# Eighteen small unused GpSimd loads beside a softmax that keeps VectorE and the DMA engines full

## The chip, the cores and the metric

One core of a Trainium2 chip. The metric is device microseconds of one execution of the whole program. A span in the profile is the same execution by the profiler's clock, about 1.8 us shorter.

## The reference

Softmax over the last axis of a float32 array of 16 x 1024 x 512, with temperature 0.5:

```python
def reference(x):
    temp = 0.5
    x_scaled = x / temp
    x_max = np.max(x_scaled, axis=-1, keepdims=True)
    exp_x = np.exp(x_scaled - x_max)
    return (exp_x / np.sum(exp_x, axis=-1, keepdims=True)).astype(np.float32)
```

33.55 MB are read and 33.55 MB written; the arithmetic is small beside that.

## The kernel before

The 16,384 rows are cut into eight chunks of 128 partitions x 16 rows x 512 (4.19 MB each). Six buffers hold chunks; the loads of the last two chunks wait until the stores of the first two have left theirs. VectorE takes the maximum and makes the bias, ScalarE the exponentials with their sums, VectorE the reciprocal and the product (ScalarE takes an eighth of that), and a store in place follows. Loads go out on SyncE's queue, stores on ScalarE's.

```python
    def load(c):
        if c < BUFS:
            chunks[c] = data.tile([P, G, D], fp32, name="xt")
        else:
            chunks[c] = chunks[c - BUFS]
        xt = chunks[c]
        for lo, hi in LOADS[c]:
            nc.sync.dma_start(out=xt[:, lo:hi, :], in_=xr[c][:, lo:hi, :])
    # ... shift, exponentials, scale_vector, scale_scalar: the arithmetic of one block
    def store(i):
        c, _, end = blocks[i]
        for lo, hi in STORES[c]:
            if hi == end:
                nc.scalar.dma_start(
                    out=outr[c][:, lo:hi, :], in_=chunks[c][:, lo:hi, :]
                )
    # ... the pipeline over 11 blocks: shift two ahead, exponentials one ahead, store(i) last
```

## Time and profile before

| | before |
|---|---|
| time, median of 2 runs | 162.37 us (162.31 to 162.43) |
| span of the profiled run | 160.6 us |
| VectorE busy | 134.6 us (84%) |
| DMA engines, both big queues | 97.7% of the span |
| last store issued / its landing time | 147.55 us / 12.2 us |

One group more matters later, from the groups of instructions of the kernel before (busy us, mean ns, then idle time ahead of it): the bias, which is the one VectorE operation that could meet GpSimd.

```profile
L78 DVE TENSOR_SCALAR bias<-negmax 128x16 f32<-128x16 f32 (+2 forms) x11 | 1.9, 173 | 0.4
```

### The profile page before, as it was taken

The page shows a single profiled execution, that of the slowest core. Times are in us where ns is not written, and L with a number is a line of the kernel's source. Part 1 is how long each engine was busy: PE and PEld are TensorE (multiplying, and loading weights), DVE is VectorE, ACT ScalarE, POOL GpSimd, SP SyncE. Part 2 cuts the span into 40 slices and gives each one's busy share as a digit, 9 for nine tenths or more (in the row PEclk, how much of TensorE's full clock was granted, in tenths as well). Part 3 has the DMA queues.
Part 4 walks back from the last instruction along what each step waited for, and adds up shares of the span by engine and source line. Part 5 has one row for each costly group of instructions (what it writes and reads, how often), then busy time and mean ns, then how long its engine had stood idle before and what let it go on. Part 6 is the DMA issues. An engine that isn't in the chain of part 4 may idle for free.

```text
span 160.6 us, 402 instructions
## 1 busy us (share of the span) xinstructions
DVE 134.6 (84%) x45; ACT 102.1 (64%) x273; POOL 0.2 (0%) x4
## 2 busy tenths in 40 slices
DVE  0507999999999999999999999999999999957000
ACT  3071549069979963998199909991899891790000
POOL 0000000000000000000000000000000000000000
DMA  5999999999999999999999999999999999999993
GB/s 182 471 400 506 400 400 498 408 392 484 424 400 384 400 457 449 400 441 465 400 424 473 408 408 492 400 392 498 416 392 490 424 392 457 457 392 449 465 392 139
DMA packets 2450, 67.13 MB, mean 418 GB/s; under 512 B 272, under 2 KB 272, under 8 KB 272
## 3 DMA queue, kind: packets, MB, share of 16 engines
q1 hardware_dynamic: 1296, 33.56, 49.3%
q10 hardware_dynamic: 1152, 33.55, 48.4%
q14 instruction: 2, 0.02, 0.0%
HBM read 33.55 MB, written 33.55 MB: 418 GB/s over the span
## 4 chain that ended last, share of the span: by engine, by line
DVE 80%; DMA 7%; ACT 4%; issue 0%; SPq 0%
DVE negmax L74 42%; DVE xt L102 36%; DMA xt<-in_x_dram 7%; ACT xt L85 4%; DVE bias L78 1%; DVE recip L100 1%; SPq L66 0%
## 5 line engine op out<-in xcount | busy, mean ns | idle before, releaser
L85 ACT ACTIVATE xt<-xt,bias 128x512 f32<-128x512 f32 x128 | 90.4, 708 | 41.7 <-DVE bias L78 41.2
L74 DVE TENSOR_REDUCE negmax<-xt 128x16 f32<-128x8192 f32 (+2 forms) x11 | 69.9, 6352 | 9.5 <-DMA xt<-in_x_dram 9.5
L102 DVE TENSOR_TENSOR xt<-xt,recip 128x7168 f32<-128x7168 f32 (+2 forms) x11 | 62.0, 5637 | 0.4
L85 ACT ACTIVATION_READ_ACCUMULATOR xt<-xt,bias 128x1 f32 x128 | 23.9, 187 | 0.0
L111 ACT ACTIVATE xt<-xt,recip 128x512 f32<-128x512 f32 x15 | 9.9, 706 | 0.0
L100 DVE RECIPROCAL recip<-sums 128x16 f32<-128x16 f32 (+2 forms) x11 | 2.4, 218 | 1.8 <-ACT xt L85 1.8
L78 DVE TENSOR_SCALAR bias<-negmax 128x16 f32<-128x16 f32 (+2 forms) x11 | 1.9, 173 | 0.4
L52 ACT ACT_TABLE_LOAD x1 | 1.3, 1283 | 0.7 <-PEq L148 0.7
L51 DVE MEMSET warm<- 128x1 f32 x1 | 0.1, 59 | 0.8 <-PEq L148 0.8
L52 ACT ACTIVATE warm<-warm 128x1 f32<-128x1 f32 x1 | 0.2, 203 | 0.0
L148 POOL MEMSET const-bfloat16-1.0<- 128x1 bf16 x1 | 0.1, 103 | 0.0
L148 POOL MEMSET const-uint8-127<- 128x1 uint8 x1 | 0.1, 103 | 0.0
L148 POOL MEMSET const-float32-1.0<- 128x1 f32 x1 | 0.1, 100 | 0.0
L148 POOL MEMSET const-float32-0.0<- 128x1 f32 x1 | 0.1, 99 | 0.2 <-issue 0.2
## 6 DMA issues: line engine op xcount, KB each, us to landing
out_dram<-xt ACTq DMA_DIRECT2D x8, 4096.0 KB, 22.8
xt<-in_x_dram SPq DMA_DIRECT2D x7, 4096.0 KB, 30.2
xt<-in_x_dram SPq DMA_DIRECT2D x1, 3072.0 KB, 11.7
xt<-in_x_dram SPq DMA_DIRECT2D x1, 1024.0 KB, 4.9
```

Source lines behind the costliest of these rows:

```text
L51: nc.vector.memset(warm, 0.0)
L52: nc.scalar.activation(out=warm, in_=warm, func=EXP)
L74: nc.vector.tensor_reduce(negmax[:, 0:b], chunks[c][:, lo:hi, :], axis=AX, op=MAX, negate=True)
L78: nc.vector.tensor_scalar_mul(biases[i][:, 0:b], negmax[:, 0:b], 2.0)
L85: nc.scalar.activation(out=row, in_=row, func=EXP, bias=biases[i][:, g : g + 1], scale=2.0, accum_out=sums[i][:, g : g + 1],)
L100: nc.vector.reciprocal(recips[i][:, 0:b], sums[i][:, 0:b])
L102: nc.vector.tensor_mul(rows, rows, recips[i][:, 0:k].unsqueeze(2).broadcast_to((P, k, D)))
L111: nc.scalar.activation(out=row, in_=row, func=COPY, scale=recips[i][:, g : g + 1])
L148: nc = _bacc.Bacc("TRN2", target_bir_lowering=False, num_devices=1)
```

## The change

It adds loads that no one reads, each of the six in a round of a size of its own, so that they can be told apart in a record of DMA packets. They are called markers here. Each round has markers of 2, 4 and 8 partitions with one row each, and of 1, 1 and 14 partitions with two rows each. Nothing else is touched.

```diff
         xt = chunks[c]
+        if c in (1, 5, 6):
+            mark_pool()
         for lo, hi in LOADS[c]:
             nc.sync.dma_start(out=xt[:, lo:hi, :], in_=xr[c][:, lo:hi, :])
+
+    junk = stats.tile([16, 2, D // 2], fp32, name="junk", bufs=1)
+
+    def first(n, size):
+        nc.gpsimd.dma_start(out=junk[0:n, 0, 0:size], in_=xr[0][0:n, 0, 0:size])
+
+    def turn(n, size):
+        nc.gpsimd.dma_start(
+            out=junk[0:n, :, 0:size], in_=xr[0][0:n, 0:2, 0:size]
+        )
+
+    def mark_pool():
+        first(2, 250)
+        first(4, 240)
+        first(8, 230)
+        turn(1, 220)
+        turn(1, 210)
+        turn(14, 200)
```

## The prediction

> **What bounds the kernel now.** I read the page first (busy shares, the row of slices, DMA queues), then the chain that ended last, then the landing times of the DMA issues, and last the stretches of the tail. From the page:
>
> ```profile
> span 160.6 us, 402 instructions
> DVE 134.6 (84%) x45; ACT 102.1 (64%) x273; POOL 0.2 (0%) x4
> DVE  0507999999999999999999999999999999957000
> POOL 0000000000000000000000000000000000000000
> DMA  5999999999999999999999999999999999999993
> DMA packets 2450, 67.13 MB, mean 418 GB/s; under 512 B 272, under 2 KB 272, under 8 KB 272
> q1 hardware_dynamic: 1296, 33.56, 49.3%
> q10 hardware_dynamic: 1152, 33.55, 48.4%
> ```
>
> Two rows are full at once. VectorE is at 9 from the fifth slice to the 35th, and the DMA engines are at 9 from the second slice to the 39th. The two queues together take 49.3 + 48.4 = 97.7% of the engines' time. GpSimd does nothing after four constants. So there are two candidates for the bound, and the chain tells which one sets the end:
>
> ```profile
> DVE 80%; DMA 7%; ACT 4%; issue 0%; SPq 0%
> 1.15 11.71 DMA xt<-in_x_dram
> 12.88 2.30 DVE negmax L74
> 143.59 3.89 DVE xt L102
> ```
>
> VectorE starts in earnest at 12.88 us, when the second load of the first chunk lands, and goes on to 147.48 us (143.59 + 3.89) with one wait of 1.8 us for ScalarE. Then the last store goes out. What follows is pure DMA:
>
> ```profile
> 147.55 0.34 ACTq L119 DMA_DIRECT2D out_dram<-xt  x1
> DMA to landing us min/median/max: 12.2/22.8/32.4
> xt<-in_x_dram SPq DMA_DIRECT2D x1, 1024.0 KB, 4.9
> 144.00:146.00 2.00, 2.00 (x1) 0.54 (x1) 0.00 (x0) 1.00 0.76 328
> ```
>
> The second line is the least, middle and longest landing time of the eight stores, each 4.194 MB; 147.55 + 12.2 = 159.75, against a span of 160.6, so the shortest is that of the last store. Set beside the very first load, which found the engines empty (1.049 MB, 4.9 us), it gives a straight line: (12.2 - 4.9) / (4.194 - 1.049) = 2.32 us per MB, or 431 GB/s, and 4.9 - 1.049 x 2.32 = 2.5 us that do not depend on size. The last store therefore found no backlog that this line would show, and the DMA share of 0.76 just before it says the same. Conclusion: the end is the first load (12.88) + VectorE's chain (134.6) + one store alone (12.2) and about 1 us around them. The DMA engines are a near second: they finish what was queued just as the last store arrives, so a DMA loss over the whole run has hardly any slack to hide in.
>
> **What the Trainium skill says.** First, "DMA: Bandwidth & Descriptors", section "Why a DMA increments its semaphore by 16 and not by 1": a DMA issued by GpSimd has all 16 engines post the completion, whatever its shape, while its data go to k consecutive engines from a cursor that moves on. The trace agrees on the 16 as far as it goes: 17 DMAs x 16 = 272, just the count of packets under 512 B. The cursor, no line of the kernel before shows. Second, same page, "Queues, rings and completion order": each engine goes round its queues packet by packet. In the trace a data packet is a 32 KB row (33.55 MB over 1,024 rows in q10), which at 431 / 16 = 26.9 GB/s takes 1.22 us; that is my unit for one turn of another queue. Third, same page, "Anatomy of one DMA": a GpSimd DMA costs some 2.0 us fixed, mostly completion; my line has 2.5 us for the other queues. Fourth, "SBUF — State Buffer", section "Who interferes with whom": descriptor generation on GpSimd is kept out, or keeps VectorE out, only where VectorE is in a mode that uses both port pairs, which tensor_reduce and tensor_tensor are not said to have; a tensor_scalar can. Here that is the 11 small multiplications that make the bias, 0.17 us each. No run here shows such a conflict yet.
>
> **The change, part by part.** It removes nothing and moves nothing. VectorE, ScalarE and SyncE have the same instructions with the same waits in the built program; only GpSimd gets 18 DMAs. It looks as if the three rounds belonged to the loads of chunks 1, 5 and 6, but GpSimd has no wait on these loads. All 18 write the same scratch tile, so each but the first waits for the completion of the one before, and nothing else. The series starts right after the start barrier, near 0.8 us, and runs on by itself; no one waits for it except the end of the kernel.
>
> *Bytes.* One round: 2 x 1000 + 4 x 960 + 8 x 920 + 2 x 880 + 2 x 840 + 28 x 800 B = 39,040 B in 46 rows. Three rounds: 0.117 MB in 138 rows, 0.17% of 67.13 MB. At 431 GB/s that is 0.27 us if spread evenly. If the cursor works as the skill says, a round covers 2 + 4 + 8 + 2 + 2 + 14 = 32 shares, each engine twice, so evenly it is.
>
> *Packets.* 138 data and 18 x 16 = 288 completions = 426 on top of 2450, or 27 per engine beside 153. What does a small one cost? The only hint before: q1 has 144 packets more than q10 for 0.01 MB more, and 0.9% more of the engines' time, which is 0.009 x 160.6 x 16 / 144 = 0.16 us each. Most of these 144 are the first chunk's extra data rows, and one queue reads HBM while the other writes it, so this is a ceiling. With 0.02 us each (my choice, an estimate), 27 make 0.5 us per engine; the ceiling would make 4.3 us.
>
> *On the path.* About a tenth of the series runs before 12.88 us, so the first load loses some 0.05 us. VectorE's chain loses time only if a bias multiplication meets descriptor generation. Taking 1 us of GpSimd per DMA (estimate), 18 us in 160 is a chance of 0.11 each; 11 x 0.11 x about 0.5 us = 0.6 us if every overlap blocked, and I count a third, 0.2 us. The DMA loss of 0.27 + 0.5 us is hidden while VectorE sets the pace and reaches the end only as backlog in front of the last store; I count a third, 0.25 us. Sum: 0.05 + 0.2 + 0.25 = 0.5 us, so 162.37 + 0.5 = 162.9 us.
>
> **The rivals.**
> *The series outlasts the kernel.* A marker that lands slowly makes the 18 in series long. Its time is 2.5 us fixed, about 1 us to make descriptors, and turns behind 32 KB packets: until the first store at 45.6 us only loads are queued (1.22 us a turn), later both queues (up to 2.44 us). If a marker's rows and completion go as one packet, that is 4.7 to 5.9 us, and the series ends near 18 x 5.5 = 99 us, far from the end. If each row and the completion need a turn of their own, up to three turns, it is 7.2 us early and up to 10.8 us late: six markers by 45 us, twelve more at 8.5 us on average, end near 147 us. The edge is 160 / 18 = 8.9 us each. Above it, markers are left when the last store lands, each at about 3.5 us: at 10 us each two are left, +7 us, about 169 us (4% slower). For it: both queues are full nearly throughout. Against: waits for a whole turn on every descriptor are the worst case. I give it 0.13.
> *Small packets cost their ceiling.* 4.3 us per engine, not hidden because the engines are full: about 166 us, 2% slower. Against: 272 such packets are there already without denting the 0.98 to 1.03 shares of the middle stretches. Weight 0.04, half of it past 2%.
> *Wholly hidden.* The markers fill gaps, VectorE feels nothing, 162.4 us. The likeliest neighbour of my figure, 0.4.
> *Faster?* Nothing is removed, and no order changes; only chance in which queue goes first could gain, tenths of a us. 0.01.
>
> **Range and chances.** Same within 2% is 159.1 to 165.6 us. From the above: slower 0.13 x 0.7 + 0.04 x 0.5 = 0.11, rounded to 0.12 for an added fixed cost of a third queue at the end of the program, which I cannot size; faster 0.01; within 2% 0.87. The range that should hold it 8 times in 10 is lopsided for the same reason: 162.2 to 165.2 us, and the figure is 162.9 us.
>
> **What would show it.** In the profile after: 426 more packets (2876), all under 2 KB, in a third queue with well under 1% share; 288 of them under 512 B. VectorE's groups keep their times (tensor_reduce of 8192 elements 8.68 us, the multiplication of 7168 7.63 us), and bias near 0.17 us with at most one or two stretched. The last store is issued within 1 us of 147.55 and lands in 12.2 to 13 us. The markers land in 5 to 9 us each and the last before 150 us. I am wrong if the chain of work ends in a marker or in GpSimd; if VectorE shows new idle time before a group; if the last store lands in more than 14 us; or if the loads of the first chunk land over half a us later than 12.88.

## The result, and the profile after

163.62 us (163.56 to 163.68, 2 runs) against 162.37 us: ratio 1.0078, interval 1.0058 to 1.0098. A ratio is the mean time of one kernel's fast runs over that of the other's of the same rounds, so not quite the ratio of the medians quoted. The time is inside the range forecast, 0.7 us above the figure.

The page after, the lines that answer to those in the prediction:

```profile
span 161.9 us, 424 instructions
DVE 134.6 (83%) x45; ACT 102.1 (63%) x273; POOL 10.1 (6%) x22
DMA packets 3026, 67.25 MB, mean 415 GB/s; under 512 B 752, under 2 KB 848, under 8 KB 848
q1 hardware_dynamic: 1296, 33.56, 49.0%
q10 hardware_dynamic: 1152, 33.55, 48.0%
q0 software_dynamic: 576, 0.12, 0.4%
L100 DVE TENSOR_SCALAR bias<-negmax 128x16 f32<-128x16 f32 (+2 forms) x11 | 1.9, 173 | 0.4
```

VectorE's 134.6 us and the bias's 173 ns have not moved: GpSimd didn't hold VectorE up. The new queue q0 has 576 packets, not the 426 of the prediction, and 0.4% of the engines' time. 576 is 18 x 32. The packet records of the trace, which give sizes and times but don't name the engines, show where they come from: 96 packets carry rows, and 480 have 4 or 8 bytes. 18 x 16 = 288 of the small ones are the completions; that leaves 192, and 96 + 192 = 288 is again 16 per marker. So it looks as if each engine that got no row got a small filler packet instead.

The chain of waits after, the store's landing times (least, middle, longest) and the markers' landing times:

```profile
1.16 11.76 DMA xt<-in_x_dram
143.64 3.89 DVE xt L124
DMA to landing us min/median/max: 13.0/24.2/33.4
DMA to landing us min/median/max: 4.9/7.3/9.8
136.98 0.62 POOL L78 DMA_DIRECT2D junk<-in_x_dram  x1 [6.97 <-DMA junk<-in_x_dram]
```

The first chunk lands at 12.92 in place of 12.86 us, and VectorE ends at 147.53 in place of 147.48. The last store is the one with the least landing time, and that rose from 12.2 to 13.0. The 18 markers ran one behind the other and the last was issued at 137.0 us, so the series was over at 144.7 us, before the kernel's end.

That leaves a part which neither chain shows: after the last store had landed. This is SyncE in the trace records, start times in us, from the last landing to the end:

```
before  landed 159.71  waits 159.77 159.83                                            end barrier 159.89  span ends 160.57
after   landed 160.57  waits 160.58 160.65 160.71 160.77 160.83 160.89 160.95 161.01 161.08  end barrier 161.14  span ends 161.90
```

A completion semaphore is a counter that a DMA raises when its data have landed. The program ends with SyncE waiting for every one that was used, up to two of them in one instruction. The first start listed for the changed kernel is that of the wait which the last store ends; the same one of the kernel before is not in its line, because its record starts at 140.43 us. Behind that wait stand two more before and eight after. In the new kernel eight semaphores belong to GpSimd's markers; they had been full for about 16 us, yet six waits with one of them stand behind the last store's, and each takes 0.06 us although there is nothing to wait for. From the last landing to the end it is 0.85 us before and 1.33 us after: 0.39 us of the difference lies before the end barrier, in these waits, and 0.08 us in the barrier itself (0.67 us before, 0.76 after), where GpSimd's clearing of the semaphores takes 0.14 us in place of 0.09.

So the span's 1.33 us come apart like this, each from one profile:

| part | before | after | difference |
|---|---|---|---|
| last store issued | 147.55 | 147.61 | +0.06 |
| last store to its landing (records) | 12.16 | 12.96 | +0.80 |
| last landing to the end of the span | 0.85 | 1.33 | +0.47 |

The packet records also tell why the landing moved. In the kernel before, from 5 us to the issue of the last store, each engine was without a packet for only about 0.1 us in all, so there was no gap in which the markers could hide. In the changed kernel their packets took 0.60 us an engine, and the ends of the last 16 rows, averaged, moved from 158.35 to 159.07 us, by 0.72. The difference of 0.12 is within the scatter: in the run *one* below, with 0.02 us of marker packets, that average is 158.71 us.

### The profile page after: what moved, and what is told of

The parts are those of the page before. It is cut to its first block, busy times and chain, and to the rows that moved or that the text cites. A ratio compares the mean times of both kernels' runs of the same rounds, so it can differ in the third digit from the quotient of the medians.

```text
span 161.9 us, 424 instructions
## 1 busy us (share of the span) xinstructions
DVE 134.6 (83%) x45; ACT 102.1 (63%) x273; POOL 10.1 (6%) x22
## 4 chain that ended last, share of the span: by engine, by line
DVE 79%; DMA 7%; ACT 4%; issue 0%; SPq 0%
DVE negmax L96 41%; DVE xt L124 36%; DMA xt<-in_x_dram 7%; ACT xt L107 4%; DVE bias L100 1%; DVE recip L122 1%; SPq L68 0%
## 5 line engine op out<-in xcount | busy, mean ns | idle before, releaser
L78 POOL DMA_DIRECT2D junk<-in_x_dram x9 | 5.0, 553 | 66.8 <-DMA junk<-in_x_dram 66.8
L75 POOL DMA_DIRECT2D junk<-in_x_dram x9 | 4.9, 543 | 60.5 <-DMA junk<-in_x_dram 59.6
```

What stands on the lines that cost most here:

```text
L75: nc.gpsimd.dma_start(out=junk[0:n, 0, 0:size], in_=xr[0][0:n, 0, 0:size])
L78: nc.gpsimd.dma_start(out=junk[0:n, :, 0:size], in_=xr[0][0:n, 0:2, 0:size])
```

## The experiments

**Theories.** A: the DMA engines are a full second bound, so the markers' engine time comes back nearly whole at the last store, and the end waits come on top. B: the slow series, still running near the end, is what hurts; early losses would be made up. C: a third queue costs a flat sum as soon as it is used. Two more came up with the results, D (a burst among loads alone puts the engines out of step) and E (the uneven share of rows does). Runs of one call were taken on the same chip with 11 runs of the kernel before (medians 162.27, 162.33 and 162.33 us in the three calls).

| run | median us | ratio (interval) | VectorE ends | last store to landing | landing to end |
|---|---|---|---|---|---|
| before (first profile) | 162.37 | | 147.48 | 12.16 | 0.85 |
| changed (first profile) | 163.62 | 1.0078 (1.0058 to 1.0098) | 147.53 | 12.96 | 1.33 |
| again | 163.57 | 1.0084 (1.0070 to 1.0098) | 147.46 | 13.48 | 1.33 |
| one | 162.53 | 1.0018 (1.0002 to 1.0035) | 147.24 | 12.51 | 0.99 |
| same8 | 163.18 | 1.0057 (1.0041 to 1.0073) | 147.50 | 12.22 | 1.32 |
| burst18 | 164.14 | 1.0111 (1.0098 to 1.0124) | 147.66 | 13.38 | 1.33 |
| late18 | 163.68 | 1.0089 (1.0074 to 1.0103) | 147.35 | 13.06 | 1.33 |
| even18 | 163.59 | 1.0076 (1.0064 to 1.0088) | 148.06 | 12.36 | 1.32 |
| merged | 163.03 | 1.0044 (1.0031 to 1.0058) | 148.68 | 11.50 | 0.99 |
| short (wrong) | 161.21 | 0.9928 (0.9917 to 0.9940) | 147.28 | 11.10 | 0.85 |
| shortmarks (wrong) | 161.81 | 0.9969 (0.9957 to 0.9981) | 147.58 | 11.10 | 1.32 |

The last three columns are of one profiled run each, from its trace records, so they scatter by some tenths. The first profile of the changed kernel and that of *again* differ by 0.5 us in the landing time alone, and *again* was profiled in its slowest run (164.12 us).

**again**: no edit.

> The changed kernel once more, with enough rounds to give an interval. Theory A (engine time and end waits): the DMA engines are never idle, so each of the 32 packets per marker, two per engine, pushes the last store back (about 0.6 to 0.9 us in all), and SyncE waits for seven more semaphores one after the other at the very end (0.061 us each, 0.43 to 0.48 us in all). Sum +1.2 to +1.4 us. Every theory must give back +1.25 us here.

+1.36 us by the ratio (0.0084 x 162.3). It repeats, and its end part is again 1.33 us.

**one**: a single marker.

```diff
-        if c in (1, 5, 6):
+        if c == 1:
             mark_pool()
     def mark_pool():
-        first(2, 250)
-        ... (five more)
+        nc.gpsimd.dma_start(out=junk[0:2, 0, 0:250], in_=xr[0][0:2, 0, 0:250])
```

> A single marker of 2 partitions in place of 18. Theory A: 32 packets, 0.02 to 0.05 us of engine time, at most one more semaphore at the end, so +0.05 to +0.15 us. Rival C (a third queue costs a flat sum as soon as it is used at all): +1 us or more.

+0.29 us, interval +0.03 to +0.57. C's flat +1 us is out. The figure is above A's 0.05 to 0.15, which still lies within the interval. The end part is 0.99, that is 0.14 more than without any marker: 0.06 for one wait more, and the 0.08 of the end barrier, which is the same with one marker as with 18. So a small flat part does exist.

**burst18**: the same markers, but each into partitions of its own, so that the wait for the one before is gone without a race.

```diff
-    junk = stats.tile([16, 2, D // 2], fp32, name="junk", bufs=1)
+    junk = stats.tile([P, 2, D // 2], fp32, name="junk", bufs=1)
+    used = [0]
     def first(n, size):
-        nc.gpsimd.dma_start(out=junk[0:n, 0, 0:size], in_=xr[0][0:n, 0, 0:size])
+        a = used[0]
+        used[0] = a + n
+        nc.gpsimd.dma_start(out=junk[a : a + n, 0, 0:size], in_=xr[0][0:n, 0, 0:size])
     # turn likewise
```

> The same 18 markers, each into its own partitions of the scratch tile, so that none waits for the one before (up to eight in flight); they are through within the first third of the kernel. Theory A: same packets, same semaphores, so +1.2 to +1.4 us like the changed kernel. Rival B (what hurts is a slow series that still disturbs single engines near the end, so that they finish apart): early losses are made up before the last store, the engines end together again, and only the end waits are left, +0.5 us.

+1.80 us (+1.59 to +2.01; the 1.87 in later expectations is the difference of the medians). The last marker was issued at 26.8 us and the last landed at 45.4. B is out: the loss is not made up in the 115 us that follow. But A's 1.2 to 1.4 was missed from the other side, by about half a microsecond; the next three runs ask why.

**same8**: eight markers of the smallest kind.

```diff
     def mark_pool():
-        first(2, 250)
-        ... (five more; and the three rounds are one)
+        for k in range(8):
+            nc.gpsimd.dma_start(
+                out=junk[2 * k : 2 * k + 2, 0:250], in_=xr[0][0:2, 0, 0:250]
+            )
```

> Eight markers of the smallest kind (2 partitions, one row) at once, so all eight GpSimd semaphores are used but there are only 16 packets per engine. Theory A: end waits in full, 0.43 to 0.48 us, plus 0.15 to 0.25 us of engine time, +0.6 to +0.75 us. If the end waits cost nothing: +0.2 to +0.3 us. Rival C: +1.2 us.

+0.92 us (+0.67 to +1.18); A's 0.6 to 0.75 reaches only into the lower edge of the interval. The end part is full, 1.32 us, with eight markers as with 18: it goes with the eight semaphores, not with the number of markers.

**late18**: the burst held back to about 90 us by a VectorE memset of one column of the scratch tile.

```diff
+        if i == 7:
+            nc.vector.memset(junk[:, 0, 0:1], 0.0)
+            mark_pool()          # three rounds at once, written as in burst18
```

> The 18 markers in a burst again, but held back by a small VectorE memset until about 90 us, when loads and stores share the engines. Theory A: engine time is lost alike wherever it falls, and the end waits stay, so +1.2 to +1.4 us, and the early burst's +1.87 us would be chance. Theory D (an early burst, among loads alone, puts the engines out of step, and they never come to rest to fall in step again, so that one engine ends late): the late burst costs less than the early one, near the series' +1.3 us or below, and the last rows of the engines end closer together.

+1.44 us (+1.20 to +1.67), beside +1.80 for the early burst and +1.36 for the series. The direction is D's, but the intervals of the two bursts overlap by 0.08 us. The late burst is also drawn out: beside loads and stores its markers were issued from 87.6 to 125.4 us.

**even18**: an early burst in which every engine gets one row of every marker.

```diff
+        for k in range(18):
+            a = 16 * (k % 8)
+            nc.gpsimd.dma_start(
+                out=junk[a : a + 16, k // 8, :], in_=xr[0][0:16, 0, 0:100]
+            )
```

> 18 markers in an early burst, each of 16 partitions and 400 B a row, so that every engine gets one row of each; about the same bytes and just the same 576 packets as the changed kernel. Theory A: +1.2 to +1.4 us. Theory E (the uneven share of rows, 2, 4 or 8 engines at a time, is what makes the burst worse): clearly under burst18's +1.87 us. If the early burst as such is what costs: +1.8 us again.

+1.23 us (+1.04 to +1.43), clear of burst18. The early burst as such isn't what costs more, and E fits. It pays elsewhere: the first chunk lands later, as the chain of this run shows, and the store takes 12.36 us in return.

```profile
1.16 12.29 DMA xt<-in_x_dram
144.17 3.89 DVE xt L115
```

The first chunk lands at 13.45 us, 0.59 later than before, and VectorE ends 0.58 later. (Leaving out merged, the other runs have it between 12.64 and 13.06.)

**same64**: the loop of same8 with 64.

> 64 markers of the smallest kind at once, eight times as many as in the run with eight, with the same eight semaphores at the end. Theory A by the recorded packet times (0.18 us an engine for eight): 1.45 us and 0.48 us of end waits, +1.9 us. If each marker costs as much as the series shows beyond the end waits (0.82 us for 18): 2.9 + 0.5, +3.4 us. If the engines had slack to make it up: +0.5 us.

171.31 us, ratio 1.0549: none of the three figures. The run was ill-chosen, because 64 markers are made at one per 2.5 us and outlast the kernel; the chain says so, and the last ones go out after the stores are done:

```profile
DMA junk<-in_x_dram 91%; POOL junk L76 2%; POOLq L171 0%; PEldq L171 0%
163.00 0.52 POOL L76 DMA_DIRECT2D junk<-in_x_dram  x1 [1.94 <-DMA junk<-in_x_dram]
```

It still gives the slope, from the packet records: the ends of the last rows, averaged over the engines, are 158.36 us with eight markers and 159.66 with 64, so +1.30 us for 56 markers. The recorded times of their packets rose by 1.469 - 0.181 = 1.29 us an engine, of which 1.13 lie before 158.4 us. So engine time given to markers comes back about one to one; that the figures agree more closely is luck, as this average scatters by 0.36 us between *before* and *one*.

**serial24**: a fourth round in the series.

```diff
-        if c in (1, 5, 6):
+        if c in (1, 2, 5, 6):
             mark_pool()
```

> A fourth round in the series (24 markers in place of 18). The prediction's first rival, made to happen: the changed kernel's 18 markers ended at 144.7 us, the last three at 7.4 us each, so two more fit before the stores are through at about 160 us, and four are left at 2.5 to 4 us each on idle engines. The kernel should end at 170 to 176 us by its own clock, +9 to +14 us, and the chain should end in the markers. Theory A alone without this (only occupancy): +0.3 us more than the changed kernel.

171.11 us, ratio 1.0537 (1.0521 to 1.0552), span 169.5 us: just under the 170 to 176 expected, because the last three markers on idle engines followed each other at some 2 us. The chain of this run ends in them:

```profile
150.49 7.79 DMA junk<-in_x_dram
158.56 2.72 DMA junk<-in_x_dram
161.56 1.64 DMA junk<-in_x_dram
163.48 0.52 POOL junk L78
```

A marker takes 7.8 us here beside full engines, and the last four take 1.6 to 2.7, where the stores end or have ended (the last row at 160.78 us). The rival of the prediction was real; 18 markers stay below it and 24 do not.

**short**: the kernel before with half of the last chunk not loaded. The result is wrong in those rows (relative error 0.238), on purpose: it takes 2.1 MB from the engines and nothing from VectorE.

```diff
-    LOADS = [[(0, 4), (4, G)]] + [WHOLE] * 7
+    LOADS = [[(0, 4), (4, G)]] + [WHOLE] * 6 + [[(0, 8)]]
```

> The kernel before with half of the last chunk's load left out (2.1 MB less to read, so 4.9 us less for the engines at 431 GB/s); wrong in those rows on purpose. It gives the DMA engines slack. Theory A: the last store can't start before VectorE is done, so nearly nothing is gained, -0.5 to +0.1 us, and the engines idle before the last store. If the engines alone set the end: up to -4 us.

-1.17 us (ratio 0.9928), more than the -0.5 to +0.1 expected and far from the -4 of a pure DMA bound. **shortmarks** is the changed kernel with the same edit.

> The changed kernel with the same half load left out; wrong on purpose in the same rows. Theory A: with slack on the engines the markers' engine time is absorbed and only the end waits are left: +0.4 to +0.6 us over the run without markers. If the markers cost by something else than engine time at a full engine: +1.25 us over it again.

161.81 us, that is +0.60 us over short by the medians, where the markers cost 1.25 to 1.36 us with full engines. The stretch just before the last store (us and length, busy VectorE, ScalarE and GpSimd, clock, DMA share, GB/s), first of short, then of shortmarks, then of the kernel before, then of the changed kernel:

```profile
146.00:147.40 1.40, 1.28 (x1) 0.00 (x0) 0.00 (x0) 1.00 0.00 0
```

```profile
146.00:147.40 1.40, 1.40 (x1) 0.00 (x0) 0.00 (x0) 1.00 0.01 0
```

```profile
146.00:147.40 1.40, 1.40 (x1) 0.00 (x0) 0.00 (x0) 1.00 1.19 515
```

```profile
146.00:147.40 1.40, 1.40 (x1) 0.00 (x0) 0.00 (x0) 1.00 0.92 398
```

In the first two no big packet starts in that stretch; in the last two the engines are still at older work (a share counts a packet where it starts, so in short stretches it swings). Then the landing times of the stores, of short and of shortmarks:

```profile
DMA to landing us min/median/max: 11.1/20.4/29.7
```

```profile
DMA to landing us min/median/max: 11.1/21.1/30.2
```

With slack the last store takes 11.1 us with markers and without. The markers' engine time is gone from the end; what is left is the end waits (1.32 against 0.85 us) and a first chunk that landed 0.3 us later (12.96 against 12.67 us, about as much as it varies between other runs). This is the run that carries theory A.

**merged**: the bytes of all 18 in one load.

```diff
+    junk = stats.tile([16, 1830], fp32, name="junk", bufs=1)
+    def mark_pool():
+        rows = xr[0].rearrange("p g d -> p (g d)")
+        nc.gpsimd.dma_start(out=junk, in_=rows[0:16, 0:1830])
```

> The bytes of all 18 markers (0.117 MB) in one GpSimd load of 16 partitions: 32 packets, one semaphore. Theory A: 0.3 us of engine time by the bytes, 0.14 us at the end as in the run with one marker, +0.3 to +0.5 us. If the bytes were what costs: +1.2 us.

+0.71 us (+0.50 to +0.94): half the cost for the same bytes, but more than A's 0.3 to 0.5. The packets' own time is 0.36 us an engine and the end part 0.99. But this load sits in front of the first chunk with all its bytes at once:

```profile
1.16 12.91 DMA xt<-in_x_dram
144.79 3.89 DVE xt L112
```

The chunk lands at 14.08 us, 1.2 us later than before, and VectorE's whole chain shifts by that, to 148.68. The packets' 0.36 us alone don't make 1.2: in the records the chunk's own rows of 24,576 bytes, 8 an engine, also took 1.015 us each in place of 0.912, which is 0.8 us more; why is open. The engines caught up meanwhile: 15 of them had run out of packets before the store's rows began, and the store took 11.5 us. Here VectorE has become the bound. In the changed kernel it was the DMA engines.

**What stays open.** That burst18 costs about half a microsecond more than even18 is measured; against the series the intervals just touch, and against late18 they overlap a little. That the uneven rows put single engines behind is only argued. One pair of profiles fits: the last 16 rows end at 159.15 us on average in burst18 and at 159.13 in even18, but the latest of them at 160.76 against 160.14. The series has a late one too, though (160.67 in *again*). In the packet records the engines end their last rows apart: in the kernel before 15 of them between 158.15 and 158.53 us and one at 159.36; in short, where all engines had been idle before the last store, all 16 between 157.95 and 158.11. This fits the idea that a microsecond lost on one engine stays until the engines come to rest, but two profiles don't show it. Which packet put that one engine behind, the records don't say, since they don't name engines. The same scatter may be why runs and profiles of one program differ by some tenths.

## Why the prediction was right or wrong

The time was in the range and, as forecast, within 2%; the added cost was 1.25 us where 0.5 was forecast. By its steps:

- *What bounds the kernel.* Half right. "The last store therefore found no backlog that this line would show" was the weak point: the line took 2.5 us without bytes from the first load, and short shows that a store with the engines idle takes 11.1 us: 8 rows an engine of 1.21 us each, 9.7 us, and 1.4 us. So 1.06 of the 12.16 us were backlog, most of it on one engine: 15 began the store's rows between 148.41 and 148.85 us, the last not before 149.61 (in short all 16 between 148.20 and 148.36). The DMA share of 0.76, read as a sign of rest, was such a swing; the next stretch, below, has 1.10, and by the packet records all 16 engines were at work through both. The DMA engines, called "a near second", were level with VectorE. No run shortens VectorE's chain to tell how far they alone would hold the end.

```profile
146.00:148.00 2.00, 1.48 (x1) 0.00 (x0) 0.00 (x0) 1.00 1.10 475
```

- *The packets.* The count failed (426 forecast, 576 found): 192 fillers came on top, and the two rows of a partition in the marker of 14 went as one packet, 42 fewer. The 16 completions a DMA were right, though the 272 named for them belong to SyncE's and ScalarE's DMAs and say nothing of GpSimd's. The size was close: 0.27 + 0.5 = 0.77 us an engine forecast, 0.60 recorded. The small completion and filler packets took 9 ns each, not 20.
- *"I count a third, 0.25 us."* This is the term that failed most in the sum. Nothing was hidden: the last store took 0.80 us longer to land, for 0.60 us of packets; the engines had only about 0.1 us each of idle time to hide them in; and shortmarks shows that with engines at rest the loss is gone. The store's 13.0 us is at the edge of the 12.2 to 13 forecast, and the 13.5 of *again* is outside.
- *The bias, 0.2 us.* Nothing: 173 ns before and after, and no new idle time on VectorE. The GpSimd instructions took 0.52 to 0.67 us, not 1 us.
- *The first load, 0.05 us.* It fits, 12.86 to 12.92 us, but is smaller than the scatter: 12.67 and 12.72 us in short and late18, which have no marker at that time.
- *The end of the program.* Named only as a cost "which I cannot size"; it is 0.47 us, over a third of the whole. The kernel before shows 0.06 us for each wait behind the last store's, so 8 x 0.06 = 0.48 us could have been estimated.
- *The rivals.* The series stayed clear of the end, with landing times of 4.9 to 9.8 us for the 5 to 9 forecast. The working behind the edge (number of markers times landing time against 160 us) was fair: 24 markers of 6 to 9 us cross it and cost 8.8 us.

Two terms too high (the bias; bytes and packets together, by 0.17 us) and two too low (the share that isn't hidden, the end waits) left 0.5 forecast against 1.25 measured. The range held it because it was drawn longer upwards, in part for the end cost that had no size. The page "DMA: Bandwidth & Descriptors" of the Trainium skill, section "Issuing engines are not separate DMA queues", has the principle that decided it: a load of GpSimd shares the 16 engines with all others. The trace agrees: ScalarE's last store lands 0.80 us later behind markers that GpSimd issued.

## What to carry to other kernels

In this kernel, whose DMA engines never come to rest, small transfers cost their engine time in full (0.60 us of packets, 0.80 us at the last store), even early ones (burst18) and although no one waits for them; a test that gives the engines slack shows this better than a busy share does. Count semaphores as well as bytes: eight more of them cost 0.47 us here at the very end, mostly as waits on things long done. The same bytes in one transfer cost 0.71 us in place of 1.25 to 1.36, and most of that came from lying in front of the load that VectorE waits for first.

## What the Trainium skill lacked or had wrong

- "DMA: Bandwidth & Descriptors", section "Why a DMA increments its semaphore by 16 and not by 1", says that all 16 engines post a completion for a GpSimd load; the runs agree (the 32 packets of merged are 16 rows and 16 of 4 bytes). It lacks the further small packets, one for each engine without a row by the count: 32 packets for every marker with 1 to 16 partitions (576 for 18, 32 for one, 2048 for 64). A filler or completion took 9 ns.
- The same page, section "Anatomy of one DMA": a fixed cost of about 2 us. Idle engines agree (a marker in 1.6 to 2.7 us at the end of serial24); beside full engines the same loads took 4.9 to 9.8 us, which that section doesn't give.
- None of the pages that I read has the cost of waiting at the end of a program for semaphores that were full long before: 0.06 us for each wait; from last landing to end 0.85 us with none of GpSimd's, 0.99 with one, 1.33 with eight, of which 0.08 us is a longer end barrier.
- None of them has it that the 16 engines end apart when they have not rested: last rows 1.2 us apart in the kernel before, 0.16 us in short, where they had rested.
